# Attention on one core: four late pairs of heads transposed by DMA inside SBUF, loads issued earlier, and a seventh exponential group on VectorE

## The chip, the cores and the metric

The kernel runs on one core of one Trainium2 chip. The metric is the device time of one execution in microseconds; where a set of runs is given, it is the median. A core has five engines that run side by side, each with its own instruction queue in program order: TensorE (PE in the profile), VectorE (DVE), ScalarE (ACT), GpSimd (POOL) and SyncE (SP), which in this kernel issues nearly all DMAs.

## The reference

Softmax attention over 64 heads (8 batches of 8), each with 512 queries, 512 keys and 64 dimensions, in fp32:

```python
scale = 1.0 / np.sqrt(q.shape[-1])
scores = np.einsum('bhqd,bhkd->bhqk', q, k) * scale
scores = scores - scores.max(axis=-1, keepdims=True)
attn = np.exp(scores)
attn = attn / attn.sum(axis=-1, keepdims=True)
return np.einsum('bhqk,bhkd->bhqd', attn, v).astype(np.float32)
```

## The kernel before

**Tiling.** Two heads make a pair; there are 32 pairs, numbered 0 to 31. For one pair, q, k and v are loaded as three fp32 tiles of 128 partitions x 512 (256 KB each, `load`, line 317). GpSimd casts k and q to fp16 into one tile `qkp` of [128, 2, 4, 128] (`cast_qk`, line 334) and v into `vp`, which has an extra column of ones (`cast_v`, line 329). TensorE transposes the eight 128x128 blocks of `qkp` into a PSUM bank `tp` (line 357), and VectorE copies them to `tqk` in SBUF (`copy`, line 364), so that the 64 dimensions lie on the partitions.

**Scores and exponentials.** A block is 128 keys against all 512 queries of one head. Two blocks, usually one of each head, make a group; there are 129 groups, numbered 0 to 128, four to a pair, the last two being single blocks. `scores` (line 368) multiplies a group into one of three PSUM buffers `st`. ScalarE then takes the exponential of the group's 1024 columns into an fp16 tile `pt` (line 388). There is no subtraction of the maximum. For a few groups VectorE computes the exponential instead: `raise_` (line 402) turns the scores into a power of two in fixed point, `z`, which frees the `st` buffer, and six passes split it into mantissa and exponent (lines 415 and 426) and evaluate a polynomial (line 437, four times, the last of them writing `pt`).

**Values.** For 128 queries of one head, a unit, TensorE adds up four products of `pt` with `vp` into one of seven places of an output tile `o` in PSUM (`values`, line 462, matmul at 471). The column of ones gives the sum of the exponentials. When seven units are full, VectorE takes the reciprocals (line 449) and multiplies (line 450) into a ring of 56 units in SBUF (`normalise`), from which SP stores each completed head (line 458). The output tiles and the transposed pairs share two PSUM banks, `x0` and `x1`.

**What sets the order.** The order of every engine is fixed before the kernel is built. The class `Plan` (line 17) steps through a model of TensorE, ScalarE and VectorE in steps of 5 ns with durations written at its head, and writes down the order in which TensorE takes scores, transposes and values, and VectorE takes raises, copies, norms and passes; ScalarE follows the scores. The constants at line 43 steer it: `LATE_NORM` and `LATE_COPY` are how far ahead of a pass's end another job may fall due without holding the pass back; `SOON` and `BACKLOG` decide when TensorE waits for a score buffer rather than taking other work. Line 44: the last `LAST_PAIRS` pairs have no group on VectorE; a new group may be raised when at most `AHEAD` passes are left; `MARGIN` stretches the passes' durations; `SLACK` is added to the time at which a VectorE group's values are taken to be ready; `MOST` is the highest number of groups on VectorE.

**Feeding.** With the first group of each pair g, `feed(g)` (line 346) is emitted: it issues the loads of pair g+5 on SP, and the casts of k and q of pair g+3 and of v of pair g+2 on GpSimd. Pairs 0 to 4 are loaded at the start (lines 611 to 617). The pools hold six load tiles of each of q, k and v, three `qkp` and four `tqk`. `HALVED` (line 284) names the pairs whose v load is issued as two halves. Every DMA signals one of eight semaphores in turn, so that a DMA is not issued before the one eight places ahead has landed.

Of the kernel before, what the change touches and what calls it, by code (L numbers as in the profile page):

```python
# [16 lines left out]
class Plan:  # L17
# [11 lines left out]


    SLOT, EXP, EXP_DONE, EXP_FIXED = 216, 853, 181, 64
    INTO, OUT_OF = 95, 105
# [9 lines left out]

    LATE_NORM, LATE_COPY, HURRY, SOON, BACKLOG = 200, 200, 900, 220, 1000
    LAST_PAIRS, AHEAD, MARGIN, SLACK, MOST = 2, 0, 1.1, 2000, 6

    def __init__(self, groups, pairs, first):
# [5 lines left out]
        for m in range(first):  # L52
            self.act += self.EXP + self.EXP_FIXED
            self.exps[m] = self.act + self.EXP_DONE
            self.read.append(self.exps[m])
        self.tq = {0: 5800}
        self.next_t = 1
# [118 lines left out]
    def step_pe(self, t):  # L176
        if self.m == len(self.groups):
            self.values(t)
            return
        g = self.groups[self.m][0][0]  # L180
        backlog = self.act - t
        one, two = self.free() <= t, self.free(1) <= t
        if one and (two or backlog < self.HURRY or self.tiled):
            return self.scores(t)
        if not one and backlog < self.BACKLOG and self.free() < t + self.SOON:
            return
        if self.part_t:
            return self.transposes(t)
        if (
            self.next_t < self.pairs  # L190
            and self.next_t <= g + 1
            and t >= self.ready_kq(self.next_t)
            and self.bank(t) is not None
        ):
            return self.transposes(t)
        if not self.values(t) and one:
            self.scores(t)
# [44 lines left out]
def kernel(  # L242
# [28 lines left out]
    cpool = ctx.enter_context(tc.tile_pool(name="const", bufs=1))  # L271
    lpool = ctx.enter_context(tc.tile_pool(name="load", bufs=6))
    qpool = ctx.enter_context(tc.tile_pool(name="qk16", bufs=3))
    tpool = ctx.enter_context(tc.tile_pool(name="tqk", bufs=4))
    ppool = ctx.enter_context(tc.tile_pool(name="pt", bufs=30))
# [7 lines left out]

    HALVED = range(20, 25)
    NU = 56
# [20 lines left out]
    def load_tile(g, name):  # L306
# [4 lines left out]
            name=f"{name}32_{g}",  # L311
            bufs=6,
        )
# [20 lines left out]
    def cast_qk(g):  # L334
# [9 lines left out]
        qkp[g] = t  # L344

    def feed(g):
        load(g + 5, "kqv")
        cast_qk(g + 3)
        cast_v(g + 2)
# [260 lines left out]
    with tc.manual_schedule():  # L610
        first_loads()
        load(1, "kq")
        load(0, "v")
        for g in range(2, 5):
            load(g, "kq")
            load(g - 1, "v")
        load(4, "v")
        make_identity(nc, ident)
# [50 lines left out]
```

## Time and profile before

| | |
|---|---|
| median of 8 runs | 123.15 us (122.81 to 123.60) |
| the profiled execution, its own time | 123.46 us |
| its span in the profile | 121.7 us |
| ACT, exponentials of line 388 | 120, 109.5 us busy |
| DVE, polynomial passes of line 437 | 24, from 16.0 to 105.2 us |
| PE, transposes of line 357 | 248, 19.7 us busy |
| DVE, copies of line 364 | 30, 20.6 us busy, 687 ns each |
| POOL, casts of lines 332 and 340 | 612 ns at least, 1668 ns at most |
| DMA | 33.82 MB, mean 278 GB/s |
| median from issue to landing, us | k 4.7, q 4.9, v 5.3, store of one head 3.9 |
| time in which SP waits to issue stores, for DVE | 18.5 us behind the multiply, 4.4 us behind the reciprocal |

The profile is one execution recorded on the chip. A busy time is the time in which an engine had an instruction under way, so pipelined instructions that overlap count once; a mean duration of one instruction may therefore be longer than the distance from one to the next. A row of waits gives the engine and line that waited, the engine and line that it waited for, and the total in us, the count and the longest in us. The chain of work that ended last is followed back from the last instruction to whatever released it; "issue" in it is time in which an engine waited for nothing that the profile shows. A stretch given as A:B is in us from the start of the span; its columns are the busy us of the engines with their counts of instructions, then the granted clock of TensorE, the share of time of the DMA engines and GB/s.

### The profile page before, as it was taken

What the parts mean: (1) busy time and instruction counts of PE and PEld (TensorE: products, weight loads), DVE (VectorE), ACT (ScalarE), POOL (GpSimd) and SP (SyncE); (2) the same over time, 40 slices, a digit from 0 to 9 for tenths busy, and PEclk for the clock granted to TensorE, in tenths of its full rate; (3) what the DMA queues carried; (4) which work ended last, traced back from release to release, by engine and by line L of the source; (5) the groups of instructions that cost most, each with busy time, mean ns of one, the idle gap of its engine ahead of it and who ended that gap; (6) DMA issues with size and microseconds to landing.
All of it is one profiled execution on the core that took longest, in us unless ns stands there. A gap on an engine that the chain in (4) does not pass through costs nothing.

```text
span 121.7 us, 3953 instructions
## 1 busy us (share of the span) xinstructions
PE 103.4 (85%) x1557; PEld 65.3 (54%) x1557; DVE 98.3 (81%) x171; ACT 114.4 (94%) x127; POOL 74.1 (61%) x101
## 2 busy tenths in 40 slices
PE   7967888879898899878899889988989987898970
PEld 2633546447465567544565556656555754576450
DVE  1547699999998989988997988889898998846261
ACT  4698999999999999999999999999999999999970
POOL 2358999997599394953596787356885646200000
PEclk9999999999999999999999999999999999999998
DMA  3899999999999998999899999999997994033253
GB/s 114 270 368 384 379 378 382 383 356 301 276 327 320 315 288 259 297 364 330 255 340 287 358 333 293 320 267 298 291 359 260 289 336 165 0 112 109 93 167 94
DMA packets 35603, 33.82 MB, mean 278 GB/s; under 512 B 2688, under 2 KB 35584, under 8 KB 35584
## 3 DMA queue, kind: packets, MB, share of 16 engines
q1 hardware_dynamic: 35152, 33.24, 84.2%
q10 hardware_dynamic: 432, 0.33, 0.8%
q8 instruction: 12, 0.20, 0.7%
q14 instruction: 7, 0.06, 0.2%
HBM read 25.17 MB, written 8.39 MB: 276 GB/s over the span
## 4 chain that ended last, share of the span: by engine, by line
ACT 60%; issue 17%; PE 13%; DMA 4%; SPq 1%; DVE 1%; POOL 1%; ACTq 0%
ACT pt L388 60%; PE st L383 7%; DMA v<-in_v_dram 4%; PE o L471 4%; PE tp L357 1%; SPq L327 1%; SPq L515 1%; DVE tqk L364 1%; POOL vp L332 1%; DVE obl L499 0%; PE o_last L486 0%; DVE rc_last L498 0%; ACTq L388 0%
## 5 line engine op out<-in xcount | busy, mean ns | idle before, releaser
L388 ACT ACTIVATE pt<-st 128x1024 f16<-128x1024 f32 (+1 forms) x120 | 109.5, 1266 | 0.6 <-PE st L383 0.6
L383 PE MATMUL st<-tqk 64*128 64x512 f16 x248 | 45.8, 382 | 10.2 <-ACT pt L388 8.0
L471 PE MATMUL o<-vp,pt 128*128 128x65 f16 x1008 | 41.8, 194 | 0.5 <-POOL vp L332 0.5
L471 PEld LDWEIGHTS <-pt 128*128 128x128 f16 x1008 | 35.8, 98 | 11.7 <-issue 11.2
L340 POOL CAST qkp<-k 128x512 f16<-128x512 f32 x31 | 24.7, 795 | 23.9 <-DMA k<-in_k_dram 15.4
L332 POOL CAST vp<-v 128x512 f16<-128x512 f32 x32 | 27.1, 848 | 0.8 <-DMA v<-in_v_dram 0.7
L383 PEld LDWEIGHTS <-tqk 64*128 64x128 f16 x248 | 12.7, 93 | 26.3 <-issue 19.3
L364 DVE COPY tqk<-tp 128x1024 f16<-128x1024 f16 x30 | 20.6, 687 | 6.4 <-PE tp L357 5.6
L340 POOL CAST qkp<-q 128x512 f16<-128x512 f32 x30 | 23.9, 795 | 2.4 <-DMA q<-in_q_dram 2.1
L450 DVE TENSOR_TENSOR ring<-o,rc 128x448 f32<-128x448 f32 (+2 forms) x37 | 22.6, 611 | 1.3
L357 PE MATMUL tp<-ident,qkp 128*128 128x128 f16 x248 | 19.7, 220 | 2.9 <-DVE ring L450 1.3
L357 PEld LDWEIGHTS <-qkp 128*128 128x128 f16 x248 | 14.1, 97 | 10.8 <-POOL qkp L340 6.2
L437 DVE SCALAR_TENSOR_TENSOR y<-y,m 128x1024 f32<-128x1024 f32 x12 | 16.7, 1389 | 0.0
L449 DVE RECIPROCAL rc<-o 128x7 f32<-128x7 f32 (+2 forms) x37 | 7.3, 196 | 5.8 <-PE o L471 5.3
L437 DVE SCALAR_TENSOR_TENSOR pt<-y,e 128x1024 f16<-128x1024 f32 x6 | 8.4, 1393 | 0.1
L437 DVE SCALAR_TENSOR_TENSOR y<-m 128x1024 f32<-128x1024 f32 x6 | 8.4, 1398 | 0.0
L402 DVE TENSOR_SCALAR z<-st 128x1024 uint32<-128x1024 f32 x6 | 7.3, 1217 | 1.2 <-PE st L383 1.2
L426 DVE TENSOR_SCALAR e<-z 128x1024 uint32<-128x1024 uint32 x6 | 4.4, 740 | 0.0
L415 DVE TENSOR_SCALAR m<-z 128x1024 uint32<-128x1024 uint32 x6 | 4.1, 690 | 0.0
L519 PE MATMUL st_0a<-const-bfloat16-1.0 128*128 128x512 bf16 (+1 forms) x11 | 3.5, 484 | 0.8 <-PEq L653 0.8
L519 PEld LDWEIGHTS <-const-bfloat16-1.0 128*128 128x128 bf16 x15 | 1.7, 131 | 2.4 <-issue 2.4
L535 ACT ACT_TABLE_LOAD x1 | 1.3, 1283 | 1.7 <-PEq L653 1.7
(43 smaller groups left out, 17.7 us busy)
## 6 DMA issues: line engine op xcount, KB each, us to landing
out_dram<-ring SPq DMA_DIRECT2D x63, 128.0 KB, 3.9
k<-in_k_dram SPq DMA_DIRECT2D x31, 256.0 KB, 4.7
q<-in_q_dram SPq DMA_DIRECT2D x31, 256.0 KB, 4.9
v<-in_v_dram SPq DMA_DIRECT2D x27, 256.0 KB, 5.3
v<-in_v_dram SPq DMA_DIRECT2D x10, 128.0 KB, 4.1
k<-in_k_dram ACTq DMA_DIRECT2D x2, 128.0 KB, 2.8
q<-in_q_dram SPq DMA_DIRECT2D x2, 128.0 KB, 2.6
out_dram<-obl SPq DMA_DIRECT2D x1, 64.0 KB, 1.6
```

The lines of the kernel that those rows point to most:

```text
L332: nc.gpsimd.tensor_copy(out=vps[g % NV][:, :, :, 0:D], in_=raw[g]["v"][:, :, :, :])
L340: eng.tensor_copy(out=t[:, n].rearrange("p i (h d) -> p h i d", h=2), in_=raw[g][name][:, :, :, :],)
L357: nc.tensor.transpose(tps[g][:, n, i, :], qkp[g][:, n, i, :], ident)
L364: nc.vector.tensor_copy(out=tqk[g][:, :, :], in_=tps.pop(g).rearrange("p n i c -> p n (i c)"))
L383: nc.tensor.matmul(st[:, x, :], kc, qc, start=True, stop=True)
L388: nc.scalar.activation(out=pt[:, 0:size, :], in_=st[:, 0:size, :], func=EXP, scale=scale)
L402: nc.vector.tensor_scalar(out=r["z"][:, :, :], in0=r["st"][:, :, :], scalar1=scale * 1.4426950408889634 * 2.0**23, scalar2=(127 + SHIFT) * ...
L437: nc.vector.scalar_tensor_tensor(out=r["pt"][:, :, :] if n == 3 else r["y"][:, :, :], in0=mant if n == 0 else r["y"][:, :, :], scalar=QUAR ...
L449: nc.vector.reciprocal(out=rc[:, 0:n], in_=o[:, x : x + n, D : D + 1])
L450: nc.vector.tensor_tensor(out=ring[:, u % NU : u % NU + n, :], in0=o[:, x : x + n, 0:D], in1=rc[:, 0:n].broadcast_to([P, n, D]), op=AluOp. ...
L471: nc.tensor.matmul(os[u // 7][:, u % 7, :], blocks[(g, c, h)][:, y * P : (y + 1) * P], vps[g % NV][:, h, c, :], start=(c == 0), stop=(c == ...
L519: nc.tensor.matmul(dst[:, 0:n], ones[:, 0:P], ones[:, 0:n], start=True, stop=True)
```

## The change

Pairs 19, 22, 25 and 28 are no longer transposed by TensorE and copied by VectorE. `feed(g)` first issues, for pair g+5 if it is one of them, one DMA on SP's queue that transposes the whole `qkp` tile into `tqk`. The planner takes these pairs as ready from the start and leaves their transposes and copies out. Loads go seven pairs ahead instead of five, and pairs 0 to 6 are loaded at the start. At the feeds of pairs 8, 10 and 12 one pair more is cast, so that from pair 12 on the casts are six pairs ahead instead of three. The pools grow to eight load tiles, six `qkp` and seven `tqk`. The v loads of pairs 18, 19, 25 and 26 are halved as well. The planner may put seven groups on VectorE instead of six and has other constants. In the order that is built, VectorE's groups are 6, 17, 34, 53, 69, 86 and 101 (of pairs 1, 4, 8, 13, 17, 21 and 25) instead of 6, 23, 41, 59, 78 and 97 (of pairs 1, 5, 10, 14, 19 and 24), and the orders of TensorE and VectorE differ throughout.

```diff
--- before.py
+++ after.py
@@ -40,8 +41,9 @@
     STEP = 5
     FIRST_UNIT = 4
 
-    LATE_NORM, LATE_COPY, HURRY, SOON, BACKLOG = 200, 200, 900, 220, 1000
-    LAST_PAIRS, AHEAD, MARGIN, SLACK, MOST = 2, 0, 1.1, 2000, 6
+    BY_DMA = (19, 22, 25, 28)
+    LATE_NORM, LATE_COPY, HURRY, SOON, BACKLOG = 600, 800, 900, 80, 1000
+    LAST_PAIRS, AHEAD, MARGIN, SLACK, MOST = 5, 1, 1.05, 0, 7
 
     def __init__(self, groups, pairs, first):
         self.groups, self.pairs = groups, pairs
@@ -53,7 +55,7 @@
             self.act += self.EXP + self.EXP_FIXED
             self.exps[m] = self.act + self.EXP_DONE
             self.read.append(self.exps[m])
-        self.tq = {0: 5800}
+        self.tq = {0: 5800, **{g: 0 for g in self.BY_DMA}}
         self.next_t = 1
         self.part_t = 0
         self.banks = [5100, 5800]
@@ -177,6 +179,8 @@
         if self.m == len(self.groups):
             self.values(t)
             return
+        while self.part_t == 0 and self.next_t in self.BY_DMA:
+            self.next_t += 1
         g = self.groups[self.m][0][0]
         backlog = self.act - t
         one, two = self.free() <= t, self.free(1) <= t
@@ -269,9 +273,9 @@
     groups += [[b] for b in tail]
 
     cpool = ctx.enter_context(tc.tile_pool(name="const", bufs=1))
-    lpool = ctx.enter_context(tc.tile_pool(name="load", bufs=6))
-    qpool = ctx.enter_context(tc.tile_pool(name="qk16", bufs=3))
-    tpool = ctx.enter_context(tc.tile_pool(name="tqk", bufs=4))
+    lpool = ctx.enter_context(tc.tile_pool(name="load", bufs=8))
+    qpool = ctx.enter_context(tc.tile_pool(name="qk16", bufs=6))
+    tpool = ctx.enter_context(tc.tile_pool(name="tqk", bufs=7))
     ppool = ctx.enter_context(tc.tile_pool(name="pt", bufs=30))
     dpool = ctx.enter_context(tc.tile_pool(name="pd", bufs=3))
     wpool = ctx.enter_context(tc.tile_pool(name="work", bufs=1))
@@ -281,7 +285,8 @@
 
     NV = 12
 
-    HALVED = range(20, 25)
+    HALVED = range(18, 27)
+    SOONER = (8, 10, 12)
     NU = 56
     ring = cpool.tile([P, NU, D], FP32, name="ring")
     vps = [cpool.tile([P, 2, NI, D + 1], FP16, name=f"vp{n}") for n in range(NV)]
@@ -309,7 +314,7 @@
             FP32,
             tag=f"{name}32",
             name=f"{name}32_{g}",
-            bufs=6,
+            bufs=8,
         )
         raw.setdefault(g, {})[name] = t
         return t
@@ -343,9 +348,21 @@
             )
         qkp[g] = t
 
+    def transpose_by_dma(g):
+        if g not in Plan.BY_DMA:
+            return
+        tqk[g] = tpool.tile([P, 2, S], FP16, tag="tqk", name=f"tqk_{g}")
+        nc.sync.dma_start_transpose(
+            out=tqk[g].rearrange("p n (i c) -> p (n i) c", c=P),
+            in_=qkp[g].rearrange("p n i c -> p (n i c)"),
+        )
+
     def feed(g):
-        load(g + 5, "kqv")
-        cast_qk(g + 3)
+        transpose_by_dma(g + 5)
+        load(g + 7, "kqv")
+
+        for n in range(sum(x < g for x in SOONER), sum(x <= g for x in SOONER) + 1):
+            cast_qk(g + 3 + n)
         cast_v(g + 2)
 
     def transposes(g, n, bank):
@@ -611,10 +628,10 @@
         first_loads()
         load(1, "kq")
         load(0, "v")
-        for g in range(2, 5):
+        for g in range(2, 7):
             load(g, "kq")
             load(g - 1, "v")
-        load(4, "v")
+        load(6, "v")
         make_identity(nc, ident)
         for n in range(NV):
             nc.vector.memset(vps[n][:, :, :, D : D + 1], 1.0)
```

## The prediction

> **What bounds the kernel now.** I read the page's busy shares first, then the chain of work that ended last, then the waits, then the busy time by stretch. The shares:
>
> ```profile
> PE 103.4 (85%) x1557; PEld 65.3 (54%) x1557; DVE 98.3 (81%) x171; ACT 114.4 (94%) x127; POOL 74.1 (61%) x101
> ```
>
> ScalarE (ACT) is at 94%, and what it misses is the start and the end. The busy time by stretch of 9.5 to 117.9 us (columns PE, PEld, DVE, ACT, POOL, each with its count) says so:
>
> ```profile
> 9.50:117.90 108.40, 95.58 (x1498) 61.18 (x1494) 94.12 (x146) 108.40 (x119) 70.53 (x90) 1.00 0.88 285
> ```
>
> ACT is covered for all 108.40 us. Covered isn't unstalled, since successive exponentials overlap. The chain, in order of time, shows the unstalled step:
>
> ```profile
> 102.67 0.09 ACT pt L388
> 102.76 0.81 issue
> 103.57 0.10 ACT pt L388
> 103.68 0.80 issue
> 104.48 0.65 ACT pt L388
> ...
> 112.90 5.02 ACT pt L388 x6
> 117.92 0.05 issue
> 117.97 0.31 PE o_last L486 x4
> ```
>
> From 102.67 to 103.57 to 104.48 one exponential of 128x1024 follows the last in 0.90 us. The stretch holds 117 full ones and two halves: 118 x 0.904 = 106.7, plus about 0.4 for the last one to finish, is 107.1; 108.4 passed. So ACT is the bound, with only about 1.3 us of real stalls to win. After ACT ends, 3.8 us follow (values, norm, store) that the change leaves alone.
>
> VectorE (DVE) takes six of the groups off ACT. I asked its busy time up to the end of its sixth chain (105.2 us) and after it:
>
> ```profile
> 9.90:105.20 95.30, 87.38 (x131) 1.00 0.96 309
> 105.20:118.90 13.70, 7.30 (x19) 1.00 0.34 111
> ```
>
> and its waits up to 105.2 (us in total, times, longest):
>
> ```profile
> DVE tqk L364 <- PE tp L357: 3.2, 9, 1.0
> DVE rc L449 <- PE o L471: 2.0, 5, 0.6
> DVE z L402 <- PE st L383: 1.2, 2, 0.9
> ```
>
> DVE was idle 7.9 of 95.3 us there. It is nearly full until 105 us and half empty after: that is what a seventh group must be squeezed from.
>
> **What the Trainium skill says.** "ScalarE: Activation LUTs", section What ACT_TABLE_LOAD costs: an ACTIVATE runs one element per cycle per lane at 1.2 GHz, so 1024 elements take 0.853 us plus a fixed part; the trace agrees with its step of 0.904. "VectorE: DVE Perf Modes", section The three transpose paths: one 128x128 block by DMA is 1.309 us, by TensorE 0.390; the trace has no DMA transpose, and its eight TensorE transposes of a pair take 0.61 us together, pipelined. "DMA: Bandwidth & Descriptors", section Latency and other measured facts: a DMA transpose moves 261 GB/s in a broken-up case and 350 to 400 in a contiguous one; again nothing here to compare. "SBUF — State Buffer", section Who interferes with whom: a DVE instruction with two SBUF inputs and a GpSimd instruction that reads SBUF exclude each other for a whole instruction; the trace agrees, as casts take 0.62 us alone and 1.60 beside the chains' two-input passes.
>
> **The change, part by part.**
>
> *A seventh group on DVE.* The built order has 119 instead of 120 exponentials on ACT and raises groups 6, 17, 34, 53, 69, 86, 101 instead of 6, 23, 41, 59, 78, 97. ACT loses one full exponential, on the path: -0.904 us. DVE gains one chain: 1.217 (raise, L402) + 0.690 + 0.740 (L415, L426) + 1.398 + 2 x 1.389 + 1.393 (L437) = 8.22 us.
>
> *Four pairs transposed by DMA.* Gone are 32 TensorE transposes (4 x 0.61 = 2.4 us of PE, beside ACT's work) and four copies (4 x 0.687 = 2.75 us of DVE). Added are four DMAs of 256 KB (0.262 MB), read and written in SBUF, on SP's queue. Price of one: at least 1.0 us (0.262 MB at the 261 GB/s of the skill), at most 8 x 1.309 = 10.5 us if eight blocks go one by one. I take 2.5 us, nearer the lower end since this kernel's other DMAs overlap on the queue (4.7 us to land one load, yet 380 GB/s at 10 to 20 us), and keep both ends. Landing time is covered: it is issued five pairs before use, and a pair lasts 108.4 / 30 = 3.6 us, so 18 us. What costs is the queue. Loads and stores need 1.05 MB per pair, 290 GB/s in 3.6 us, of 380 GB/s seen at 10 to 20 us: 24% is free, 2.5 us in the three pairs between two transposes. At 2.5 us each they just fit; I cost them at nothing. Cover: a load now goes seven pairs ahead and is needed by PE about one pair before use: 6 x 3.6 = 21.6 us, less 5 for landing and 2 for casts, 14 us. Four transposes at x us slip the loads by 4 (x - 2.5), so PE starves only over x = 6.
>
> *The new wait on SP.* The transpose waits for POOL's two casts of its pair, and the stores and loads behind it on SP's queue wait too. The casts are made one feed earlier, after a load issued two feeds earlier: 7.2 us, of which 4.9 landing and 1.2 to 3.2 casting. SP may stand up to about 1 us, four times; SP's loads have 14 us of cover, and the ring of outputs holds seven pairs. Nothing on the path. The DMA eight issues later shares its semaphore and waits for its landing; with 0.45 us an issue that bites only when landing takes over 4 us, under the same cover. POOL reuses the freed cast buffers after it, several pairs later.
>
> *Loads seven ahead, casts up to six ahead, more buffers.* They work against waits of PE for casts (second line), which come from late loads (first):
>
> ```profile
> POOL qkp L340 <- DMA k<-in_k_dram: 15.4, 12, 2.1
> ...
> PEld L357 <- POOL qkp L340: 6.2, 13, 0.9
> ```
>
> These 6.2 us lie beside ACT, mostly hidden by three score banks (2.7 us of exponentials); their share of ACT's 1.3 us isn't shown. I book 0, bound: up to -0.8. Two more pairs of loads up front keep the queue full longer before the first stores, which aren't urgent: 0. Four more halved v loads: 4 x 0.45 us of SP, 0. From pair 12's feed on a cast follows its load by one feed (3.6 us) instead of two, less than the 4.7 us that a k load takes to land: POOL will wait for loads about 1 us a pair more, and the cast of v behind it in POOL's queue with it; v is needed two feeds later (7.2 us), so 0, and up to a stall of PE if POOL is more than 4 us late.
>
> *The planner's looser numbers.* They let a DVE pass start although a copy or norm falls due before its end, so DVE idles less and PE waits more for its two banks. With seven instead of six groups holding a score bank while raised, and no two microseconds of slack before a chain's values, ACT should stall a little more: 1.3 / 6 is 0.2 per group at most, plus 0.1 for tightness: +0.3 (bounds 0 to +1.3, twice the present stalls).
>
> *Does the seventh chain end in time?* Work ahead of the chain's end on DVE: 87.38 + 8.22, four copies fewer but two of the later ones (30, 31) now before it, -2 x 0.687, and two more norms, +2 x 0.82: 95.9 us, from 9.9. In the built PE order ten value units stand between the scores 122 and 123, the first four of pair 29, then those of pair 25, which need the chain. From group 123 on ACT has four full and two halves left, 4.6 us, so exponential 122 ends at 117.0 - 4.6 = 112.4 in my forecast; scores 123 must be ready then, and ahead of that stand six value units of 0.14 us (the chain of waits has eight units in 1.13), the scores' 0.39 and a hand-over that I estimate at 0.3: the chain must end by 110.9. So DVE may idle 110.9 - 9.9 - 95.9 = 5.1 us, against 7.9 now. I expect it, since four copies of PE's transposes, part of the 3.2 us of waits, are gone and the looser rule fills the gaps.
>
> Sum: -0.904 + 0.3 = -0.6. Against the profiled execution: 123.46, with span 121.7 (1.8 around it), becomes 122.9, span 121.1. The median is 0.3 lower: 123.15 - 0.6 = 122.55.
>
> **Rivals.**
> 1. *The exponential is given back as stalls.* PE, with fewer score banks free and two banks for everything else, starves ACT 0.9 us more: 123.1. For: 1.3 us of stalls exist with six groups. Against: PE is 2.4 us lighter.
> 2. *More than forecast.* Casts are no longer late, and half or more of the 1.3 us of stalls goes: -0.904 - 0.4 + nothing for tightness, about 121.9. For: the 6.2 us above. Against: ACT itself is waited for ("PE st L383 <- ACT pt L388" 8.0 us), so the banks usually cover.
> 3. *DVE becomes the bound (slower).* If its idle time stays 7.9 us, the seventh chain ends at 113.7, 2.8 after 110.9; PE stands in front of pair 25's values and ACT behind it: -0.6 + 2.8 = +2.2, or 125.35. It decides at an idle of 5.1 us, and eats the gain at 5.7. Some of it, about +1, is likelier than all: 124.1.
> 4. *The DMA transposes hold the queue (slower).* At 7.5 us each: 4 x (7.5 - 2.5) - 14 = 6 us late loads, some 128; decides at 6 us each. For: the DMA share of 50 to 90 us is 0.99. Against: it is 1.09 at 380 GB/s and 0.99 at 313, so the share doesn't say full.
>
> **How the numbers follow.** Forecast 0.42 (122.2 to 122.75), rival 2 0.20, rival 1 0.18, rival 3 0.12, rival 4 0.08. This kernel's measurement tells about 0.3% (0.37 us) from no change. Faster by over that: forecast and rival 2, less a small part of the forecast's upper edge, 0.61. Within: rival 1 and that part, 0.19. Slower: 0.20. The range: from 121.7 (rival 2 with most stalls gone) to 124.1 (rival 3's middle), leaving out rival 4, half of rival 3 and the end of rival 2: 0.17.
>
> **What would show it.** Right: 119 exponentials still 0.904 apart, stalls near 1.6 us; DVE's last L437 of group 101 ends before about 110.9, DVE idle before it at 5 us or less; each transpose lands within some 10 us, and the waits for casts on PE shrink. Wrong: a wait of PE on "pt" from DVE near 111 us (rival 3); transposes landing over 18 us after their issue, and PE waiting for tqk or for casts after 55 us (rival 4); more "ACT pt <- PE st" (rival 1).

## The result, and the profile after

The changed kernel takes 126.52 us (median of 11 runs, 123.91 to 129.9), the kernel before 123.18 beside it (32 runs, 122.53 to 124.14). The ratio of the undisturbed runs is 1.015, interval 1.011 to 1.019; it leaves out runs over 1.5% above their kernel's fastest, which are most of the changed kernel's, so the medians stand further apart (1.027); below, "less than after" compares medians, and each ratio is of the undisturbed runs. The change makes the kernel slower; the forecast said faster, 122.55, and the time lies outside its range of 121.7 to 124.1.

The profiled execution is the changed kernel's fastest, 123.91 us with a span of 121.9, against 123.46 and 121.7 before. It shows one loss that a second profile has too, but far from all that the median lost. Its busy shares (PEld is TensorE's loading of weights):

```profile
PE 100.7 (83%) x1525; PEld 63.6 (52%) x1525; DVE 104.0 (85%) x174; ACT 113.7 (93%) x126; POOL 74.9 (61%) x101
```

ACT has one instruction less and DVE is fuller, as forecast. The waits (us in total, times, longest) name what is new:

```profile
POOL qkp L345 <- DMA k<-in_k_dram: 11.5, 6, 3.1
...
PEld L374 <- POOL qkp L345: 3.5, 9, 0.7
PE o L488 <- POOL vp L337: 2.9, 4, 1.9
...
ACT pt L405 <- PE st L400: 1.6, 2, 1.2
```

PE waits for casts of q and k less than before (3.5 us for 6.2). But its value matmuls (L488) wait 2.9 us for v's cast, 1.9 of them at once. Before they waited

```profile
PE o L471 <- POOL vp L332: 0.5, 1, 0.5
```

The wait of 1.9 us reaches ACT. The timelines of ACT and of PE (start, length, what, count, and in brackets the idle time before it and who ended it):

```profile
100.01 4.87 ACT L405 ACTIVATE pt<-st 128x1024 f16<-128x1024 f32 x5
106.07 1.94 ACT L405 ACTIVATE pt<-st 128x1024 f16<-128x1024 f32 x2 [1.18 <-PE st L400]
```

```profile
102.19 0.39 PE L400 MATMUL st<-tqk 64*128 64x512 f16 x2 [0.52 <-ACT pt L405]
104.52 1.18 PE L488 MATMUL o<-vp,pt 128*128 128x65 f16 x32 [1.95 <-POOL vp L337]
105.64 0.61 PE L400 MATMUL st<-tqk 64*128 64x512 f16 x4
```

PE stands 1.95 us before 32 value matmuls. The scores behind them in its queue come late, and ACT, which runs without a gap before and after, stands 1.18. The timelines of POOL and of SP's queue (SPq) say why v is late:

```profile
97.80 0.61 POOL L337 CAST vp<-v 128x512 f16<-128x512 f32 x1
100.76 0.62 POOL L345 CAST qkp<-k 128x512 f16<-128x512 f32 x1 [2.35 <-DMA k<-in_k_dram]
101.35 1.57 POOL L345 CAST qkp<-q 128x512 f16<-128x512 f32 x1
102.87 3.84 POOL L337 CAST vp<-v 128x512 f16<-128x512 f32 x5
```

```profile
91.11 1.24 SPq L355 DMA_TRANSPOSE tqk<-qkp  x1
92.40 0.57 SPq L332 DMA_DIRECT2D k<-in_k_dram  x1
93.02 1.01 SPq L332 DMA_DIRECT2D q<-in_q_dram  x1
94.08 0.47 SPq L332 DMA_DIRECT2D v<-in_v_dram  x1
94.65 1.42 SPq L475 DMA_DIRECT2D out_dram<-ring  x3
96.11 0.52 SPq L332 DMA_DIRECT2D k<-in_k_dram  x1
```

Read them from right to left in time. The feed of pair 25 casts k and q of pair 31, six ahead, and then v of pair 27, two ahead. v of 27 was loaded long before; but POOL works in order, and the k in front of it was loaded only at 96.11 and landed 4.53 us later (the chain of waits holds both, "96.11 4.53 DMA k<-in_k_dram"). POOL idles 2.35 us for it, then spends 2.1 on k and q that nobody needs for five pairs, and only then casts the v that PE is waiting for. The k load itself stood on SP behind the transpose of pair 28, issued at 91.11 as soon as that pair's casts were done, and behind three stores (1.4 us). In the kernel before the last k load goes out at about the same time,

```profile
95.01 0.46 SPq L327 DMA_DIRECT2D k<-in_k_dram  x1
```

but there its cast comes two feeds after it, not one. The changed kernel issues this load two feeds earlier in its program and no earlier in time, and asks for it sooner.

I take as ACT's stall what the step from one exponential to the next has over 0.904 us. Before, these make 1.29 us in all, the largest 0.30. After, they make 2.92, of which 1.53 at 103.6. So -0.904 for the exponential and +1.63 of stalls is +0.7; the stretch from ACT's steady start to its last end measures 109.00 us for 108.44, +0.56, and it starts 0.32 earlier, at 9.15 for 9.47. Together +0.24, against a span longer by 0.2.

### The profile page after: what moved, and what is told of

Its sections match the earlier page's. It is cut to its first block, busy times and chain, and to the rows that moved or that the text cites. A ratio compares the mean times of both kernels' runs of the same rounds, so it can differ in the third digit from the quotient of the medians.

```text
span 121.9 us, 3881 instructions
## 1 busy us (share of the span) xinstructions
PE 100.7 (83%) x1525; PEld 63.6 (52%) x1525; DVE 104.0 (85%) x174; ACT 113.7 (93%) x126; POOL 74.9 (61%) x101
## 2 busy tenths in 40 slices
DMA packets 39891, 34.85 MB, mean 286 GB/s; under 512 B 6977, under 2 KB 39873, under 8 KB 39873
## 3 DMA queue, kind: packets, MB, share of 16 engines
q1 hardware_dynamic: 39440, 34.29, 91.1%
## 4 chain that ended last, share of the span: by engine, by line
DVE 35%; ACT 22%; PE 20%; DMA 8%; issue 8%; POOL 2%; SPq 2%; POOLq 1%; ACTq 0%
ACT pt L405 22%; DVE y L454 10%; PE st L400 9%; PE o L488 8%; DVE tqk L381 7%; DVE ring L467 6%; DMA v<-in_v_dram 4%; DMA k<-in_k_dram 4%; DVE z L419 4%; DVE pt L454 3%; DVE e L443 2%; PE tp L374 2%; POOL qkp L345 2%; DVE m L432 2%; DVE rc L466 1%
## 5 line engine op out<-in xcount | busy, mean ns | idle before, releaser
L400 PE MATMUL st<-tqk 64*128 64x512 f16 x248 | 44.9, 382 | 10.6 <-ACT pt L405 9.1
L488 PE MATMUL o<-vp,pt 128*128 128x65 f16 x1008 | 41.3, 194 | 3.6 <-POOL vp L337 2.9
L488 PEld LDWEIGHTS <-pt 128*128 128x128 f16 x1008 | 35.9, 98 | 14.0 <-issue 11.8
L345 POOL CAST qkp<-k 128x512 f16<-128x512 f32 x31 | 25.8, 833 | 25.8 <-DMA k<-in_k_dram 11.5
L454 DVE SCALAR_TENSOR_TENSOR y<-y,m 128x1024 f32<-128x1024 f32 x14 | 19.5, 1390 | 0.1
L374 PE MATMUL tp<-ident,qkp 128*128 128x128 f16 x216 | 17.3, 220 | 2.0 <-DVE rc L466 0.7
L381 DVE COPY tqk<-tp 128x1024 f16<-128x1024 f16 x26 | 17.7, 681 | 1.4 <-PE tp L374 1.4
L374 PEld LDWEIGHTS <-qkp 128*128 128x128 f16 x216 | 12.3, 97 | 9.8 <-POOL qkp L345 3.5
L454 DVE SCALAR_TENSOR_TENSOR y<-m 128x1024 f32<-128x1024 f32 x7 | 9.7, 1383 | 0.0
L419 DVE TENSOR_SCALAR z<-st 128x1024 uint32<-128x1024 f32 x7 | 8.5, 1216 | 0.4 <-PE st L400 0.4
L432 DVE TENSOR_SCALAR m<-z 128x1024 uint32<-128x1024 uint32 x7 | 6.9, 988 | 0.0
L443 DVE TENSOR_SCALAR e<-z 128x1024 uint32<-128x1024 uint32 x7 | 5.8, 829 | 0.0
## 6 DMA issues: line engine op xcount, KB each, us to landing
out_dram<-ring SPq DMA_DIRECT2D x63, 128.0 KB, 4.0
v<-in_v_dram SPq DMA_DIRECT2D x18, 128.0 KB, 4.0
k<-in_k_dram ACTq DMA_DIRECT2D x2, 128.0 KB, 2.8
q<-in_q_dram SPq DMA_DIRECT2D x2, 128.0 KB, 2.6
```

The costliest lines, as they stand in the source:

```text
L345: eng.tensor_copy(out=t[:, n].rearrange("p i (h d) -> p h i d", h=2), in_=raw[g][name][:, :, :, :],)
L374: nc.tensor.transpose(tps[g][:, n, i, :], qkp[g][:, n, i, :], ident)
L381: nc.vector.tensor_copy(out=tqk[g][:, :, :], in_=tps.pop(g).rearrange("p n i c -> p n (i c)"))
L400: nc.tensor.matmul(st[:, x, :], kc, qc, start=True, stop=True)
L419: nc.vector.tensor_scalar(out=r["z"][:, :, :], in0=r["st"][:, :, :], scalar1=scale * 1.4426950408889634 * 2.0**23, scalar2=(127 + SHIFT) * ...
L432: nc.vector.tensor_scalar(out=r["m"][:, :, :], in0=r["z"][:, :, :], scalar1=0x007FFFFF, scalar2=0x3F800000, op0=AluOp.bitwise_and, op1=Alu ...
```

## The experiments

Each was run beside the kernel before; where its times aren't given they were within 0.3% of 123.2. "After" is the changed kernel. In words, the theories that the expectations weigh are: v's cast stands behind casts for a later pair in POOL's queue (1); DVE is too full with a seventh group (2); the DMA transposes hold SP's queue or the DMA queues (3); DVE's second group comes too early (4). The last two runs set TensorE's granted clock (5) against lateness alone (6). A granted clock of 1.00 is the full one.

**v cast first, in every feed** (e1_v_first).

```diff
     def feed(g):
...
+        cast_v(g + 2)
         for n in range(sum(x < g for x in SOONER), sum(x <= g for x in SOONER) + 1):
             cast_qk(g + 3 + n)
-        cast_v(g + 2)
```

> The changed kernel with one edit: each feed casts v before k and q. Theory 1 (late casts of v: GpSimd's v cast stands behind the casts of a pair whose load was issued one feed before, so PE stands in front of its values): PE's waits for vp at line 488 (2.9 us in all, 1.9 at 102.6 us) go, ACT's stall of 1.5 us at 103.6 goes, and the time falls by at least 1.5 us to about 122.4, with a spread nearer that of the kernel before (122.5 to 124.1). Theory 2 (DVE is full with a seventh group): no change, 124 to 130. Theory 3 (the DMA transposes hold SP and the DMA queue, so loads are late): small change, under 0.5 us.

Measured: 124.79 us (124.27 to 126.79, 6 runs), 1.7 less than after but short of the 122.4 expected; ratio to before 1.011 [1.006, 1.016]. The stall at 104 is gone. But now k and q are late at the start, where they are urgent: 5.0 us of stalls, most of them before 25 us, from 9.8 us on. Between 14.9 and 21.7 us TensorE's granted clock is 0.5 as well; the run below on the old planner's numbers comes back to that. The order helps late and hurts early, which the seventh run separates.

**Casts three ahead again, transposes only two ahead** (e2_casts_three_ahead).

```diff
-    SOONER = (8, 10, 12)
+    SOONER = ()
...
-        transpose_by_dma(g + 5)
+        transpose_by_dma(g + 2)
```

> The changed kernel with its casts three pairs ahead all through, as before, and with the DMA transposes of pair g+2 instead of g+5 at feed g; loads stay seven ahead, so a load has four feeds before its cast. Theory 1: GpSimd never waits for a load, v is cast in time, about 122.5 with little spread. Theory 2: as slow as the changed kernel. Theory 3: still slow, and a DMA transpose that takes over 7 us now comes late as well, so slower than the changed kernel.

Measured: 128.66 us (126.95 to 131.7, 6 runs); ratio 1.039 [1.033, 1.045]. The expectation failed: I had moved the transposes too near to their use. The waits of PE:

```profile
PEld L400 <- DMA tqk<-qkp: 5.3, 2, 3.2
PE st L400 <- DMA tqk<-qkp: 5.0, 2, 3.1
```

The run doesn't speak on the order of casts; it shows that two pairs of lead are too few. (Four do, in e9 below.)

**Six groups on DVE** (e3_six_groups).

```diff
-    LAST_PAIRS, AHEAD, MARGIN, SLACK, MOST = 5, 1, 1.05, 0, 7
+    LAST_PAIRS, AHEAD, MARGIN, SLACK, MOST = 5, 1, 1.05, 0, 6
```

> The changed kernel with at most six groups on DVE, so group 101 goes to ACT. ACT has 120 exponentials, +0.9 us where ACT is the bound. Theory 2: DVE's 8.2 us fewer remove the stalls, so the spread goes and the time is about that of the kernel before, 123.2. Theories 1 and 3: the stalls stay, 124 to 130 plus up to 0.9.

Measured: 126.23 us (124.78 to 127.28, 6 runs); ratio 1.021 [1.015, 1.026]. It is as slow as after, with one exponential more: taking the seventh group away doesn't help, and DVE's fullness falls as the main cause. But its own loss isn't the one above: in its profile (span 123.0, the fastest of the six) the value matmuls wait for no v, ACT's stalls make 1.64 us, and 4.76 us follow ACT's last exponential, where 3.76 did before.

**No DMA transposes** (e4_no_dma_transposes): all pairs by TensorE, all else as after.

```diff
-    BY_DMA = (19, 22, 25, 28)
+    BY_DMA = ()
```

> The changed kernel with no pair transposed by DMA: TensorE and DVE do all 31, still seven groups on DVE, loads seven and casts six ahead. Theory 3: SP isn't held by four transposes (1.2 to 1.6 us each) nor by their waits for casts, loads are earlier, so the spread shrinks and the time falls to 123.5 or less although DVE has 2.75 us more to do. Theory 1: the late casts stay, as slow and spread as the changed kernel. Theory 2: DVE has 2.75 us more, so 1 to 3 us slower than the changed kernel.

Measured: 124.08 us (123.18 to 126.57, 15 runs), 2.4 less than after; ratio 1.005 [1.002, 1.008]. The last k load is issued 7.5 us before after's, and PE waits for v 0.5 us at most:

```profile
88.62 0.39 SPq L332 DMA_DIRECT2D k<-in_k_dram  x1
```

So the transposes carry most of the loss, though DMA isn't what PE waits for. (The profile has 1.5 us of stalls at 21 to 25 us of its own, in 3.41 us at a granted clock of 0.5.)

**The traffic alone** (e5_before_plus_four_transposes): the kernel before, with four transposes into a tile that nobody reads.

```diff
     def feed(g):
+        if g in (14, 17, 20, 23):
+            spare = opool.tile([P, 2, S], FP16, tag="spare", name=f"spare_{g}", bufs=2)
+            nc.sync.dma_start_transpose(
+                out=spare.rearrange("p n (i c) -> p (n i) c", c=P),
+                in_=qkp[g + 2].rearrange("p n i c -> p (n i c)"),
+            )
         load(g + 5, "kqv")
```

(With six instead of three buffers for the casts.)

> The kernel before with four DMA transposes added at the feeds of pairs 14, 17, 20 and 23 (of pair g+2's cast tile, into a spare tile that nobody reads; six cast tiles, so that nothing waits for them); TensorE and VectorE still do all their work, so nothing is saved. Theory 3 (the transposes hold SP's queue and the DMA engines; loads, stores and casts behind them slip): +1 us or more over 123.2, with more spread. Theory 1 (v cast late behind casts that go six pairs ahead) and theory 4 (the new plan leaves too little slack early, where GpSimd is full): no change, within 0.4 of 123.2.

Measured: 123.6 us (123.17 to 125.3, 22 runs); ratio 1.0028 [1.0011, 1.0045]: 0.4 us for four transposes. SP waits for casts here too, 2.2 us in all (3.3 in after). So neither the traffic nor the wait is dear where loads have more room and v is cast in time.

**The feed alone** (e6_before_with_new_feed): the kernel before, with after's loads, casts and buffers.

```diff
-        load(g + 5, "kqv")
-        cast_qk(g + 3)
+        load(g + 7, "kqv")
+        for n in range(sum(x < g for x in SOONER), sum(x <= g for x in SOONER) + 1):
+            cast_qk(g + 3 + n)
         cast_v(g + 2)
```

> The kernel before with the new feed alone: loads seven pairs ahead, casts up to six ahead from pair 12 on, the bigger pools and the halved v loads, but the old plan (six groups, old constants) and no DMA transpose. Theory 1: v is cast late behind k and q that wait for their loads, +1 us or more. Theories 3 and 4: no loss, 122.8 to 123.4.

Measured: 123.54 us (123.12 to 124.55, 12 runs); ratio 1.0042 [1.0021, 1.0062]. The feed, v behind a cast six ahead included, costs 0.3 to 0.5 us where no transpose delays the loads.

**v cast first only from pair 12 on** (e7_v_first_late), where the casts are six ahead.

```diff
+        if g >= 12:
+            cast_v(g + 2)
         for n in range(sum(x < g for x in SOONER), sum(x <= g for x in SOONER) + 1):
             cast_qk(g + 3 + n)
-        cast_v(g + 2)
+        if g < 12:
+            cast_v(g + 2)
```

> The changed kernel with v cast before k and q from pair 12's feed on, and in the old order before it. The first experiment (v first in all feeds) won 1.7 us, and its profile had 3.9 us of ACT's stalls before 25 us. Theory 1 with that cost of v first in the early feeds: faster than the first experiment, 123.3 to 124.3. If v first helped by something early, it is no better than 124.8.

Measured: 123.54 us (122.73 to 127.56, 14 runs), 3.0 less than after; ratio 1.0009 [0.9984, 1.0033]. Its timelines of POOL and of ACT in the same stretch:

```profile
99.69 0.61 POOL L337 CAST vp<-v 128x512 f16<-128x512 f32 x1
101.77 0.61 POOL L345 CAST qkp<-k 128x512 f16<-128x512 f32 x1 [1.47 <-DMA k<-in_k_dram]
103.06 0.61 POOL L345 CAST qkp<-q 128x512 f16<-128x512 f32 x1 [0.68 <-DMA q<-in_q_dram]
```

```profile
98.58 14.00 ACT L408 ACTIVATE pt<-st 128x1024 f16<-128x1024 f32 x15
```

The last k load is as late as in after (issued at 97.93), and POOL waits for it as before; but v has gone ahead, and ACT runs through. (This profile's own stalls, 1.5 us at 22 to 25 us, are early and lie in a piece at half clock.) One moved line gives back nine tenths of the loss, in the medians (3.0 of 3.3 us) and in the ratios (1.4 of 1.5%). So the order of POOL's queue is shown as the cause. That the whole 3.0 us is the one stall is not: the two profiles of after show 1.5 and 2.0 us of it.

**After once more** (e8_after_again), for a second profile.

> The changed kernel once more, for a profile of a more usual execution than the one that came with the result (123.9, the fastest of 11). Theory 3: stalls of ACT after 55 us, at the transposes, make up most of the difference; PE waits for tqk from a transpose or for casts held up behind SP. Theory 4: they lie before 25 us. Theory 1: they lie where PE waits for vp.

Measured: 125.86 and 127.79 us. The profile (span 124.1) has the same loop, later by some microseconds. Its SP, POOL and ACT:

```profile
92.84 1.24 SPq L355 DMA_TRANSPOSE tqk<-qkp  x1
94.14 0.86 SPq L332 DMA_DIRECT2D k<-in_k_dram  x1
...
97.57 0.48 SPq L332 DMA_DIRECT2D k<-in_k_dram  x1
```

```profile
103.42 1.16 POOL L345 CAST qkp<-k 128x512 f16<-128x512 f32 x1 [3.66 <-DMA k<-in_k_dram]
104.53 1.60 POOL L345 CAST qkp<-q 128x512 f16<-128x512 f32 x1
106.08 2.84 POOL L337 CAST vp<-v 128x512 f16<-128x512 f32 x5
```

```profile
101.78 4.88 ACT L405 ACTIVATE pt<-st 128x1024 f16<-128x1024 f32 x5
108.28 1.02 ACT L405 ACTIVATE pt<-st 128x1024 f16<-128x1024 f32 x1 [1.61 <-PE st L400]
```

The stall is in both profiles, 1.53 and 1.98 us. A second loss, 1.8 us of stalls between 10 and 23 us, stands only here; from 16.3 to 19.7 the granted clock is 0.5.

**Transposes four ahead** (e9_transposes_four_ahead): the transpose follows its casts by one more feed.

```diff
-        transpose_by_dma(g + 5)
+        transpose_by_dma(g + 4)
```

> The changed kernel with one number changed: at feed g the DMA transpose of pair g+4 instead of g+5 is issued, so the casts that SP waits for are one feed (3.6 us) older. Theory 3b (SP stands in front of a transpose until its pair is cast, the loads behind it slip, the casts after them wait, and the v casts behind those come late; the transposes' traffic itself is cheap, 0.4 us by the fifth experiment): SP hardly waits for casts any more, the last k load is issued before 93 us instead of 95.0 to 97.6, PE's wait for vp after 100 us goes, and the time is 123.3 to 124.5. If the traffic or SP's issue time of the transposes is what costs: no change, about 126.5.

Measured: 124.21 us (122.03 to 128.01, 14 runs), 2.3 less than after; ratio 0.999 [0.995, 1.003]. The profile has no late v (PE waits 0.6 us at most), and SP stands 0.7 us for casts before the transposes, not 3.3. But the last k load, expected before 93 us, goes out at 96.75, since the transpose of pair 28 now stands just before it; counted from ACT's steady start, 1.2 us later in this profile, that is 0.6 earlier than in after. So SP's wait matters, but not by the way expected.

**DVE's second group later** (e10_second_group_later).

```diff
-            m > 5
+            (m == 6 or m > 22)
```

> The changed kernel with the planner kept from putting any of the groups 7 to 22 on VectorE: the second one is then group 23, as in the kernel before, and there are still seven. Theory 4 (the second chain, raised at 19.4 instead of 25.7 us, falls into the time in which GpSimd is full, and takes 1.2 to 1.8 us from ACT before 25 us): these stalls go, the one near 104 us stays, so about 125.2. Without theory 4: 126.5.

Measured: 124.83 us (122.83 to 126.51, 22 runs); ratio 1.005 [1.003, 1.008]. The early stall didn't go but moved, to 24.5 us, where ACT stalls 0.8 us and PE waits for group 6's result from DVE. The stall near 104 us, which was expected to stay, isn't in this profile (PE waits for v 0.8 us at most). So with the same feed v isn't late for every order of PE's work. Inconclusive on theory 4.

**Three of these edits together** (e11_three_edits): e7, e9 and e10.

> All three edits on the changed kernel: v cast first from pair 12's feed on, transposes four pairs ahead, second group on VectorE not before group 23. If the theories 1, 3b and 4 are the causes, ACT's stalls fall to about 1.3 us, as in the kernel before, with one exponential of 0.904 us fewer: about 122.4, the spread within 1.5 us. If something else costs, it stays above 123.2.

Measured: 123.83 us (122.93 to 128.9, 22 runs); ratio 1.005 [1.003, 1.008]. The gains don't add.

**v first late and the second group later, without transposes** (e12_three_edits_no_transposes).

> As the run of three edits, but with no pair transposed by DMA: seven groups on VectorE, which makes all 31 copies (2.75 us more). It tells what the transposes are worth once nothing waits on them. If VectorE's time is what the seventh group lacks, its last chain ends some 4 us later and the time is above that of the three edits by 0.5 to 1.5 us; if the transposes save nothing that counts, the two are the same.

Measured: 124.98 us (124.18 to 125.31, 6 runs); ratio 1.015 [1.012, 1.018]. Slower than e4, which has neither edit. Not explained.

**v first late, without transposes** (e13_v_first_late_no_transposes).

> The changed kernel without DMA transposes (as the fourth experiment, 124.1) and with v cast first from pair 12's feed on (as the seventh, 123.5). If the late v casts hurt only because the transposes hold SP's loads back, v first changes nothing here: 124.1, within 0.4. If v stands too late behind k and q in any case, it gains again, to 123.3 or less. Against the seventh experiment it also prices the transposes themselves.

Measured: 123.63 us (122.7 to 124.93, 16 runs); ratio 1.004 [1.001, 1.006]. The order of v gives 0.45 us without transposes (124.08 to 123.63; by the ratios, 1.005 and 1.004, not clear of noise) and 3.0 with them (1.015 and 1.001). And with v in order the transposes are worth nothing either way: 123.54 with, 123.63 without. Neither half costs much alone; the loss is their product.

**The old planner's numbers and six groups, with the new feed, the transposes and v first late** (e14_old_plan_new_feed_transposes).

```diff
-    LATE_NORM, LATE_COPY, HURRY, SOON, BACKLOG = 600, 800, 900, 80, 1000
-    LAST_PAIRS, AHEAD, MARGIN, SLACK, MOST = 5, 1, 1.05, 0, 7
+    LATE_NORM, LATE_COPY, HURRY, SOON, BACKLOG = 200, 200, 900, 220, 1000
+    LAST_PAIRS, AHEAD, MARGIN, SLACK, MOST = 2, 0, 1.1, 2000, 6
```

> The seventh experiment (v first late, four DMA transposes five pairs ahead) with all the planner's constants of the kernel before, so six groups on VectorE: 6, 23, 41, 59, 78, 93. Theory 4b (what spread is left comes from the new plan's lack of slack, which can't take up the scatter of the first loads): the spread shrinks to that of the kernel before, about 1.5 us, at 122.9 to 123.4. If the spread comes from the transposes or the feed, it stays at 4 us or more.

Measured: 125.56 us (124.88 to 127.1, 6 runs); ratio 1.020 [1.016, 1.023]. Going back to the old numbers and six groups wins nothing: it is slower than e7. The profile shows a mechanism that I hadn't reckoned with. Busy time by stretch (columns PE, PEld, DVE, ACT, POOL, granted clock of PE, DMA share, GB/s), and PE's timeline:

```profile
52.45:55.86 3.41, 2.77 (x52) 1.88 (x49) 3.15 (x4) 3.41 (x6) 1.82 (x4) 1.00 0.91 305
55.86:59.28 3.42, 1.85 (x15) 0.51 (x11) 3.01 (x5) 3.42 (x5) 2.81 (x5) 1.00 0.99 314
59.28:62.69 3.41, 3.41 (x35) 2.33 (x34) 1.99 (x5) 2.26 (x3) 1.06 (x2) 0.50 1.06 272
```

```profile
57.23 0.39 PE L403 MATMUL st<-tqk 64*128 64x512 f16 x2 [0.52 <-ACT pt L408]
58.15 0.39 PE L403 MATMUL st<-tqk 64*128 64x512 f16 x2 [0.52 <-ACT pt L408]
59.07 0.44 PE L403 MATMUL st<-tqk 64*128 64x512 f16 x2 [0.52 <-ACT pt L408]
59.44 1.03 PE L377 MATMUL tp<-ident,qkp 128*128 128x128 f16 x8
```

Nothing was late: PE only had too little to do, 1.85 us in 3.42. Then it is granted half its clock for exactly 3.41 us, eight transposes take 1.03 us for the usual 0.61, and ACT loses 1.5 us at 59.6. "TensorE: Matmul & The Clock Gate", section Part 1: The HAM clock gate, says that the clock is set by activity in a window of 3.413 us that runs on its own, so its place against the kernel differs from run to run. The trace agrees in the length of the piece. The page's table speaks of an idle window; the window before this piece was 54% busy. Busy time alone doesn't decide it, as the part on PE's lighter load below works out. Of the twenty profiles seven have such pieces before the end (this one, e1, e2, e4, e7, e8, e12), each with stalls of ACT of 0.4 us or more in or beside it; before's and after's have none.

**Loads before the transpose in each feed** (e15_loads_before_transposes).

```diff
-        transpose_by_dma(g + 5)
         load(g + 7, "kqv")
+        transpose_by_dma(g + 5)
```

> The changed kernel with two lines swapped: each feed issues its loads before its DMA transpose, so SP's wait for the casts of the transposed pair no longer holds back the loads of that feed (only the stores behind). Theory 3b: most of what the run with transposes four pairs ahead gained (2.3 us) is gained here, 123.7 to 124.8. If the wait on SP isn't the cause: 126.5, as the changed kernel.

Measured: 124.45 us (122.59 to 128.77, 14 runs), 2.1 less than after; ratio 1.006 [1.003, 1.009]. This is the plainer test of SP's wait: the last k load goes out at 94.94 us, 1.2 earlier than in after, and v of 27 is cast at 99.92, 2.9 earlier. The loads behind the waiting transpose were what it delayed.

**e7 with the second group later and 1.5 us of slack for the first** (e16_late_second_group_with_slack).

```diff
-            m > 5
+            (m == 6 or m > 22)
...
-                    self.exps[m] = end + self.PASS_DONE + self.TO_PE + self.SLACK
+                    self.exps[m] = end + self.PASS_DONE + self.TO_PE + (1500 if m == 6 else 0)
```

> The seventh experiment with the second VectorE group not before group 23 and 1.5 us of the planner's slack before the values of the first one (the runs with a later second group had exchanged the early stall for one of 0.8 us at 24.5 us, where PE waits for VectorE's pt of group 6). Theory 4: both early stalls go, ACT's stalls are about 1.3 us, the time about 122.4 to 122.9 with less spread. Otherwise no better than the seventh, 123.5.

Measured: 123.43 us (122.03 to 125.42, 14 runs); ratio 1.000 [0.997, 1.003]. The best median of all the runs, and equal to before. Its best single runs (122.0 to 122.5) are where the forecast was; it doesn't stay there.

**More work for TensorE** (e18_after_dummies, on after; e19_late_second_group_dummies, on e16): does a fuller PE keep its clock, and does that draw the times together?

```diff
+        if m > 5:
+            busy(st[:, 0], P)
         for x, (g, c, h) in enumerate(grp):
```

(A matmul of 128 columns of constants, overwritten by the scores.)

> The changed kernel with one more matmul of 128 columns, on constants, put into each score tile from the seventh group on just before the real scores overwrite it: some 122 of them, at about 0.06 us each 7 us of TensorE's time, from 100.7 to about 108 of 122. Theory 5 (TensorE's granted clock: the change makes TensorE lighter and lets it stall, and after a stretch that is too thin it is granted 0.5 for 3.41 us): with more work in every stretch the drops become rare, the times of single runs draw together (the changed kernel's own went from 123.9 to 129.9) and the median falls from 126.5 to about 124; the profile shows no piece at 0.5 between 12 and 105 us, the late wait for v at 104 stays. Theory 6 (only what comes late costs: v's cast, SP's loop): nothing is earlier, TensorE is busier, so the median stays at 126.5 or rises to 128.

> The same extra matmuls in the kernel of run e16 (v cast ahead of k and q from pair 12, second group of VectorE later and with slack; 123.43, single runs from 122.0 to 125.4). Theory 5: the single runs draw together near e16's best, median 122.2 to 122.6, faster than before by 0.5 to 0.8%. Theory 6: nothing is late in this one that the matmuls could cure; the median stays at 123.4 or rises by up to 1 us where TensorE follows closely on ScalarE.

Measured: 128.18 us (125.24 to 131.53, 6 runs), ratio 1.019 [1.016, 1.022], and 124.6 us (123.68 to 124.99, 6 runs), ratio 1.010 [1.007, 1.012]. Each extra matmul cost 0.11 us of PE, not 0.06: PE's busy time on after went from 100.7 to 113.9 us for 122 of them. On after the spread stayed (6.3 us). But four of the six executions still had a mean granted clock of 0.970 to 0.984, so the extra work didn't keep the clock there, and the run doesn't decide on theory 5. On e16 the times drew together (6 runs within 1.3 us, 14 within 3.4 without), but near 124.6, 1.2 above e16's median. Theory 6's numbers are nearer in both.

## Why the prediction was wrong, step by step

*Loads, casts six ahead: the step that failed.* It named the right queue and gave the wrong price: "POOL will wait for loads about 1 us a pair more, and the cast of v behind it in POOL's queue with it; v is needed two feeds later (7.2 us), so 0, and up to a stall of PE if POOL is more than 4 us late". POOL was late: in the profile its waits are 2.35 us long there, and 3.66 in the second. The 7.2 us of room were not free: v is cast by the feed that issues it, after whatever k waits for, and PE reached it 1.95 us too early. e7 takes this one order away and 3.0 us go (1.4% in the ratio).

*The wait on SP: failed with it.* "SP may stand up to about 1 us, four times; SP's loads have 14 us of cover ... Nothing on the path." In the transposes' waits SP stood 3.3 us in all, 1.7 at the longest, near the estimate. The cover was the error: 14 us is what a load may be late for PE, but POOL asks for it one feed after its issue, with no cover at all, and the v behind it has what is left. A cover was counted to the last user, while the first one held up others. And the delays feed each other: a late load makes late casts, these a late transpose, and behind it stand the next loads. The last k load went from 88.6 us (e4) to 96.1 and 97.6.

*The transposes' own cost: nearly right.* 2.5 us each was taken, 1.0 and 10.5 kept as bounds. The time that packets took on the queue rises from 84.2 to 90.8% of the span with four transposes (e5; 91.1 in after, 81.5 in e4): 2.0 to 2.6 us of all 16 DMA engines for each. The issue holds SP 1.24 to 1.62 us, and the row of the DMAs reads

```profile
tqk<-qkp SPq DMA_TRANSPOSE x4, 4.5
```

4.5 us from issue to landing, 5 pairs ahead of use. "DMA: Bandwidth & Descriptors", section Latency and other measured facts, had given the lower bound (261 GB/s); with the queue full of loads no run here comes near it. "Cost at nothing" was 0.4 us (e5). Rival 4, transposes of 7.5 us that starve PE of tqk, isn't what happened: the cost is in what they wait for, not in what they take.

*DVE and the seventh chain: right.* The forecast needed 95.9 us of work to fit before 110.9. The trace up to there, and the chain's last pass (start 109.7, 1.215 long):

```profile
9.90:110.90 101.00, 95.29 (x137) 1.00 1.00 307
```

```profile
L454 DVE SCALAR_TENSOR_TENSOR pt<-y,e x1: 1215/1215/1215, 109.7 to 109.7; 128x1024 f16<-128x1024 f32 x1
```

95.3 us of work, 5.7 idle, and it ends at 110.9. So it ended just at the limit, which the late v had itself moved back by then. The chain of work that ended last lies on DVE for 35% of the span, 1% before, so DVE has little slack; but rival 3 (DVE the bound) didn't occur, and six groups are no faster (e3).

*One exponential less, and looser numbers.* 119 exponentials, as forecast. +0.3 us was booked for stalls by tightness. Without the stall at 103.6 the first profile has 1.39 us of them for 1.29, so there the term was 0.1; the second profile has 2.9 without its late stall. e16, in the median as fast as before, gives the gain back in another place. In its profile the stalls are 1.46 us, and ACT ends at 116.52 where it ended at 117.91 before. Then the last store is issued, first before and then in e16:

```profile
118.97 0.33 SPq L506 DMA_DIRECT2D out_dram<-obl  x1
117.61 0.33 SPq L526 DMA_DIRECT2D out_dram<-obl  x1
```

It goes out 1.4 us earlier, but the spans are 121.7 and 121.9. The forecast said: "After ACT ends, 3.8 us follow (values, norm, store) that the change leaves alone." That holds in after's two profiles (3.73 and 3.72), not in every variant: 3.7 to 5.4 us in the twenty profiles, 5.42 in e16. No run looked for the reason. Rival 1, the gain given back as stalls for want of score banks, is not shown.

*PE lighter by 2.4 us.* It was an argument against stalls ("PE is 2.4 us lighter"), and it has another side: e14 shows that a PE with less to do can be granted half its clock, at 1.5 us of ACT's time. What counts as less to do can be worked out from the traces, though no run was made to test it. Cut each trace into the windows of 3.413 us at whose borders the clock changes. Add up in each the columns of PE's matmuls, those of the scores at half, since they use 64 of 128 rows; a matmul on a border is shared out by time. In the twenty profiles the 27 windows after which the clock fell, nine of them before the kernel's end, hold at most 2982 such columns (e14's: 2428), and the 646 after which it stayed full at least 3170. Busy time doesn't part them, for this window of after kept the clock:

```profile
102.92:106.33 3.41, 1.81 (x38) 1.26 (x37) 2.01 (x4) 2.23 (x4) 3.41 (x6) 1.00 0.32 108
```

It is 53% busy and holds 3449. The eight transposes of a pair are 1024 columns. In the kernel before no stretch of this length from 8 to 112 us holds fewer than 3786, wherever it is laid. In after one beside the late v holds 1057, and by this count its profiled run kept the clock only because the windows lay well.

The mean clocks on record fit this. Twice what is missing from 1, times the span, estimates the time at half clock: 2.0 us in after's profiled run, all at its end, and 4.7 to 13.6 in its eleven others. It is at most 2.7 in the kernel before but for one run (5.9), and over 3.6 in three of e7's 14. The profiles have at most 3.2 at the end. So moving v also took away stretches at half clock; that these make the 1.5 us seen in the profile into 3.0 of the median is likely, and not measured by itself.

*The sum, as the runs give it.* Feed alone +0.4, traffic alone +0.4, from 123.2: 124.0. e7 has both, the seventh group and the new numbers, at 123.54: these two gain about 0.5 (worked out, not measured alone, and e14 doesn't fit: six groups with the old numbers should have been 124.0 and were 125.56). The late v adds 3.0. So, as an estimate, the gain forecast (0.6) is there to about its size, paid for by the feed and the traffic (0.8, booked at 0), with the loss on top.

*Open.* Why edits that each help don't add (e11, e12); why e14 is slow; all that spreads the single runs. In the changed kernel's executions the time tends to rise as the mean granted clock falls, from 121.9 us of span at 0.992 to 128.0 at 0.947, but a stalled PE lowers its clock as well as a low clock stalls others, and the last two runs didn't part them; and e10 went from 122.8 to 126.2 us at 1.00. That loads before transposes, added to e16, would beat before was not tried.

## What to carry to other kernels

When a step is moved ahead in an in-order queue, ask what stands behind it there: an operation that is early for its own user makes everything behind it late, and that is priced by the first urgent one, not by the moved one's own slack. Put the urgent operation first (e7), and a queue's waiting instruction behind the loads that others need (e15). Two changes that cost 0.4 us each alone cost 3 together here, where one delays what the other waits for. And a stall of TensorE was here, by the count above, also a risk to its clock.

## What was not expected of the hardware

A DMA transpose of 128x1024 in two-byte elements inside SBUF holds SP 1.24 us when nothing is waited for, where a load of 256 KB holds it about 0.5 us, and lands in 3.8 to 5.5 us beside the loads (medians of the runs). The four raise the packets from 35667 (e4) to 39891, 1056 each. TensorE's clock fell to 0.5 for 3.41 us after windows in which its matmuls, counted by columns and rows as above, came to at most 2982, and never after 3170 or more. DVE's pass that masks the mantissa (L432, one input) took 988 ns on average, 690 before; no run looked for the reason.
